# Feed-forward layers rebuilt: up projection by seven block products, hidden values through DRAM, down projection as a stage summed in PSUM

## The chip, the cores and the metric

The kernel runs on one core of a Trainium2 chip. The metric is device time in microseconds, the median of the runs; lower is better. Inputs and outputs are float32 in DRAM.

## What is computed

A two-layer model over 1024 tokens and 256 context tokens, width 1024. Each layer is a mixer (layer 0: gated recurrence and attention; layer 1: differential attention over both sets of tokens), an output projection with a gated residual, and a convolutional feed-forward network with a gated residual. The context tokens leave the model after the mixer of layer 1. The feed-forward network (hidden width 2816, that is 22 tiles of 128) is what is changed:

```python
def conv_ffn(u, w_up, conv_w, conv_b, w_down):
    a, g = jnp.split(u @ w_up, 2, axis=-1)
    g = dwconv(g, conv_w, conv_b, FFN_PAD)
    return (jax.nn.gelu(g) * a) @ w_down
```

The convolution has three taps along the tokens. `u` is the normalized, modulated residual stream; the modulation of layer 1 is itself a product of a condition vector with a 1024 x 6144 matrix, worked out in twelve chunks of 512 columns.

## The kernel before

All products of float32 values are made of float32r parts: a value is split into a high part (a cast) and a low part (the difference), and `mm3` (L113) issues three matmuls, high x high, low x high, high x low, each with a stationary operand of 128 x 128 and up to 512 moving columns. A weight unit is 128 x 1024: `unit` (L100) loads it on the SP queue into one of three `wr` buffers, casts it on POOL (`wh`) and takes the difference on DVE (`wl`).

`ffn` (L846) runs once for each layer and works on chunks of tokens whose normalized columns lie in SBUF: in layer 0 tokens 0 to 639 and then the other 640 (384 tokens and the context), in layer 1 two chunks of 512. The gate has one or two columns more in a first chunk, for the convolution. In each chunk a loop goes over eleven groups of two hidden tiles. `up(f)` loads and splits the unit of the gate and that of the value, and makes `pg` and `pa` in PSUM, each by 8 x 3 matmuls for each piece of columns; a piece has at most 512 columns, so 640 columns are two pieces of 320, 514 are 258 and 256, and 512 are one. The gate is copied by ACT, convolved in three DVE steps, passed through gelu on ACT and multiplied by `pa`; the hidden value is split into `hh` and `hl` in SBUF. `down(gi)` then multiplies the two hidden tiles with their two units of the down weights for each token tile, into `dps`; DVE multiplies that by the gate row (`dtmp`, L952), and POOL adds it to the residual tile `ht` (L953). So each token tile is evicted eleven times in a chunk. Between groups stand chunks of layer 1's modulation (`mod_chunk_dve`, L168) and the norms of the tiles of the next chunk.

`out_proj` (L767) goes before each: for each token tile 48 matmuls into `ops`, the DVE product `tmp` (L802), the POOL addition, and, three or four tiles behind in the text, the norm: `scaled` (L233: a square on ACT, a few small steps on DVE and POOL, a POOL product `xn`) and `turned` (L242: eight transposes on PE, five evictions on DVE and three on ACT). It norms only the tokens of the first chunk; the others are normed inside `ffn`. `layer1_front` (L977) follows the first `ffn`; in it the first five token tiles have their columns already.

A planner orders the instructions of these parts by their due times. Only the attention loops (L750, L1258) stand under `manual_schedule()`: there each engine and the SP queue run in the order of the text. SP issues all DMAs named here, one after another: an issue that waits holds up those behind it.

## Time and profile before

| what | us |
|---|---|
| median of three runs | 3431.25 |
| the runs | 3423.64, 3431.25, 3432.63 |
| span of the profiled execution | 3428.6 |
| busy: TensorE matmul, VectorE, GpSimd, ScalarE | 3283.1, 2523.3, 1741.2, 1097.8 |
| mean granted TensorE clock, share of full speed | 0.989 |

For the profiled execution the page gives the span alone, from its first instruction to its last; it has no time of its own beside the three runs. The span is 2.65 us under their median. The span is read in stages: about 440 us of layer 0's projections, attention to 738, output projection to 864, feed-forward to 1810, layer 1's projections to 2154, attention to 2574, output projection to 2684, feed-forward to the end. TensorE's busy time counts matmuls that overlap; what a stage costs TensorE is read from the distance between the starts of successive matmuls.

### The profile page before, as it was taken

How to read it: one execution, taken by the hardware profiler on the slowest of the kernel's cores; microseconds unless marked ns; L12 is line 12 of the kernel's file. 1: busy time of each engine (PE TensorE's matmuls, PEld its weight loads, DVE VectorE, ACT ScalarE, POOL GpSimd, SP SyncE). 2: the span in 40 equal slices, each digit the busy share in tenths (PEclk: the TensorE clock that was granted, in tenths of full speed). 3: DMA queues.
4: the chain of work that ended last, by engine and by line, in shares of the span. 5: the costliest groups of instructions: out<-in, count | busy, mean ns of one | idle time of the engine just before them, and what ended most of it. 6: DMA issues, size and time to landing. Idle time of an engine off the chain costs nothing.

```text
span 3428.6 us, 48308 instructions
## 1 busy us (share of the span) xinstructions
PE 3283.1 (96%) x18390; PEld 2840.4 (83%) x18390; DVE 2523.3 (74%) x3518; ACT 1097.8 (32%) x2126; POOL 1741.2 (51%) x1104
## 2 busy tenths in 40 slices
PE   8998989989999999999999999888889999999999
PEld 4877778877999999999997877677778888888887
DVE  6468978876777877666676784899987567677665
ACT  3355766732111111111122221677663111111010
POOL 2223578864445555445543332477773456554545
PEclk9999999999999999999999999999999999999999
DMA  7224953354523334333335445543404433333231
GB/s 260 71 75 126 290 141 94 89 149 153 178 93 111 111 99 166 107 104 108 110 110 182 121 123 142 140 128 97 135 29 169 148 101 103 102 126 105 93 98 68
DMA packets 218494, 424.41 MB, mean 124 GB/s; under 512 B 19948, under 2 KB 137708, under 8 KB 216472
## 3 DMA queue, kind: packets, MB, share of 16 engines
q1 hardware_dynamic: 216104, 413.47, 39.3%
q10 hardware_dynamic: 2160, 7.87, 0.7%
q8 instruction: 145, 2.38, 0.3%
q14 instruction: 85, 0.70, 0.1%
HBM read 335.88 MB, written 85.39 MB: 123 GB/s over the span
## 4 chain that ended last, share of the span: by engine, by line
PE 74%; DVE 15%; issue 4%; POOL 3%; DMA 2%; ACT 1%; SPq 0%; DVEq 0%; POOLq 0%; ACTq 0%
PE pg L118 5%; PE pg L117 5%; PE pg L116 5%; PE pa L117 5%; PE pa L118 5%; PE pa L116 5%; PE dps L118 5%; PE dps L117 5%; PE dps L116 5%; DVE m L1189 3%; DVE p L1205 3%; PE pj L116 3%; PE pj L118 3%; PE pj L117 3%; DVE tt L1203 2%
## 5 line engine op out<-in xcount | busy, mean ns | idle before, releaser
L90 POOL TENSOR_SCALAR wh<-wr 128x1024 fp32r<-128x1024 f32 (+3 forms) x328 | 398.7, 1222 | 763.1 <-issue 182.9
L953 POOL TENSOR_TENSOR ht<-ht,dtmp 128x1024 f32<-128x1024 f32 x197 | 506.8, 2581 | 205.9 <-DVE dtmp L952 203.7
L98 DVE TENSOR_TENSOR wl<-wr,wh 128x1024 fp32r<-128x1024 f32 (+2 forms) x328 | 505.9, 1554 | 101.1 <-POOL wh L90 101.0
L116 PE MATMUL pg<-u,wh 128*128 128x320 f32 (+4 forms) x1232 | 387.6, 315 | 0.0
L118 PE MATMUL pg<-u,wh 128*128 128x320 f32 (+4 forms) x1232 | 386.7, 314 | 0.0
L117 PE MATMUL pg<-u,wl 128*128 128x320 f32 (+4 forms) x1232 | 386.5, 314 | 0.0
L952 DVE TENSOR_TENSOR dtmp<-dps,ga 128x1024 f32<-128x1024 f32 x199 | 241.0, 1215 | 164.7 <-PE dps L118 137.0
L117 PE MATMUL pa<-u,wl 128*128 128x320 f32 (+1 forms) x1056 | 356.8, 338 | 0.0
L118 PE MATMUL pa<-u,wh 128*128 128x320 f32 (+1 forms) x1056 | 356.4, 337 | 0.0
L116 PE MATMUL pa<-u,wh 128*128 128x320 f32 (+1 forms) x1056 | 355.9, 337 | 0.0
L118 PE MATMUL dps<-wl,hh 128*128 128x512 f32 x792 | 309.4, 391 | 0.0
L117 PE MATMUL dps<-wh,hl 128*128 128x512 f32 x792 | 309.2, 390 | 0.0
L116 PE MATMUL dps<-wh,hh 128*128 128x512 f32 x792 | 308.7, 390 | 0.0
L98 POOL TENSOR_TENSOR wl<-wf,wh 128x1280 fp32r<-128x1280 f32 x64 | 221.7, 3465 | 105.8 <-ACT wh L1224 94.4
L1184 PE MATMUL S<-k,q 128*128 128x512 f32 (+1 forms) x768 | 196.4, 380 | 57.5 <-ACT p L1195 56.1
L911 ACT COPY g<-pg 128x64 f32<-128x64 f32 (+5 forms) x176 | 61.8, 406 | 576.8 <-PE pg L118 576.8
L116 PEld LDWEIGHTS pg<-u,wh 128*128 128x128 f32 x1232 | 231.8, 188 | 10.6 <-issue 1.7
L117 PEld LDWEIGHTS pg<-u,wl 128*128 128x128 f32 x1232 | 232.2, 189 | 9.0
L118 PEld LDWEIGHTS pg<-u,wh 128*128 128x128 f32 x1232 | 231.9, 188 | 7.8
L118 PEld LDWEIGHTS pa<-u,wh 128*128 128x128 f32 x1056 | 198.6, 188 | 15.7
L117 PEld LDWEIGHTS pa<-u,wl 128*128 128x128 f32 x1056 | 199.0, 188 | 15.0
L116 PEld LDWEIGHTS pa<-u,wh 128*128 128x128 f32 x1056 | 198.3, 188 | 14.5
(344 smaller groups left out, 8067.2 us busy)
## 6 DMA issues: line engine op xcount, KB each, us to landing
wr<-ffn_up SPq DMA_DIRECT2D x176, 512.0 KB
wr<-ffn_down SPq DMA_DIRECT2D x88, 512.0 KB
wr<-w_mod SPq DMA_DIRECT2D x76, 512.0 KB
k<-dk SPq DMA_DIRECT2D x14, 1280.0 KB
wr<-w_in_c SPq DMA_DIRECT2D x24, 512.0 KB
mr<-w_mod SPq DMA_DIRECT2D x20, 512.0 KB
dv<-vst SPq DMA_DIRECT2D x20, 512.0 KB
dk<-qT SPq DMA_DIRECT2D x80, 128.0 KB
```

The lines of the kernel that those rows point to most:

```text
L90: nc.gpsimd.tensor_scalar(out, x, 1.0, 1.0, op0=MUL, op1=MUL)
L98: e.tensor_tensor(out, x, hi.bitcast(F32), op=SUB)
L116: mm(out, a[0], b[0], start=start, stop=False)
L117: mm(out, a[1], b[0], start=False, stop=False)
L118: mm(out, a[0], b[1], start=False, stop=stop)
L911: nc.scalar.copy(g[:, o + lo - src:o + hi - src], pg[:, b, lo - c0:hi - c0])
L952: nc.vector.tensor_mul(tmp[:, c], ps.rearrange("p a b -> p (a b)")[:, c], gas[t0 >= SEQ][:, c])
L953: (nc.vector if last else nc.gpsimd).tensor_tensor(hts[i][:, c], hts[i][:, c], tmp[:, c], op=ADD)
L1184: nc.tensor.matmul(Y["S", m][:, c0:c0 + n], heads[h]["q"][m][:, t * P:(t + 1) * P], heads[h]["k"][x, m, j], start=(x == 0), stop=(x == 1))
L1189: nc.vector.tensor_reduce(Y["m", m], Y["S", m][:, :TOK], axis=AX.X, op=ALU.max, negate=True)
L1203: nc.vector.scalar_tensor_tensor(Y["tt"], s0[:, h, t:t + 1], self.nlam, Y["r"], op0=MUL, op1=MUL)
L1205: nc.vector.scalar_tensor_tensor(Y["p", 0], Y["p", 1], Y["tt"], Y["p", 0], op0=MUL, op1=ADD)
```

## The change

The feed-forward network becomes two stages in each layer, both wholly under `manual_schedule()`, with the hidden values of all tokens in DRAM (`hid_d`) between them.

- `out_proj` now norms every token tile. The 1024 tokens' columns are kept in float32 as four quarters `V` (half of the model's rows by half of the tokens); the context's columns are split at once (`uc`), and in layer 0 the context's tiles come first.
- `up_context` (layer 0 only) makes the hidden tiles of the 256 context tokens in the plain way, 48 matmuls of 256 columns for each. It reads all 44 units of the up weights.
- `operands` makes seven right-hand operands from the quarters, four of them by subtraction, and splits them. In layer 0 this work is handed out in pieces of 512 columns, three after each of the context's hidden tiles from the fifth on; in layer 1 in pieces of 2048 columns, in `up_begin`.
- `up_sequence` makes each hidden tile of the 1024 tokens by seven products of 12 matmuls of 512 columns (before: eight times that many columns' worth). The left-hand operands are sums of halves of the two weight units (`up_sums`, DVE). The products add up in three pairs of PSUM banks, between them ACT copies a partial sum out of the bank. The hidden tile goes to `hid_d`. In layer 0 seven chunks of layer 1's modulation stand in it.
- `ffn_down` goes over rounds of token tiles (layer 0: four, three, three; layer 1: four, four) whose sums stay in PSUM over all 22 hidden tiles. For each hidden tile it loads the unit of the down weights and the tile's tokens from `hid_d`, and splits both; three loads are ahead. A token tile is evicted once, at the end of its round. In layer 0's second and third round stand the other five chunks of modulation and the norms of the first seven tiles for layer 1.
- Both stages split weights on ACT (cast) and DVE, not POOL. `wr` has four buffers, not three; the other users of `wr` follow. `mod_chunk_dve` asks for its next load before it uses the last one. `mrow` has one buffer, not two. `layer1_front` finds seven tiles' columns made, not five.

The core of the diff (the old `ffn` is removed whole; `convolved` is its convolution, over up to 1024 columns, and `mod_steps` its modulation in six steps a chunk):

```diff
-AHEAD = 1
+NWR = 4
...
+    def place_columns(self, context):
...
+        self.V = {(i, j): pool.tile([P, 4, 512], F32, tag=f"v{i}{j}", name="v") for i in range(2) for j in range(2)}
...
+    def operands(self, U, T, n):
...
+        for k in range(0, 4, n):
+            ks = slice(k, k + n)
+            raw = {x: self.V[i][:, ks] for x, i in (("11", (0, 0)), ("12", (0, 1)), ("21", (1, 0)), ("22", (1, 1)))}
...
+            def sub(out, a, b, raw=raw):
...
+                    nc.vector.tensor_sub(raw[out], raw[a], raw[b])
...
+            def split(x, raw=raw, ks=ks):
+                return lambda: self.split(raw[x], *(y[:, ks] for y in hl[x]))
+            work += [sub("t1", "12", "11"), split("11"), sub("t2", "22", "t1"), split("t2"), split("t1"), sub("t3", "22", "12"),
+                     split("t3"), split("21"), sub("t4", "21", "t2"), split("t4"), split("22")]
...
+    def fetch_up(self, l, f):
...
+        for i in (f, NF + f):
+            raw = self.W.tile([P, 1024], F32, tag="wr", bufs=NWR, name="wr")
+            self.nc.sync.dma_start(raw, self.io["ffn_up"][l, i])
...
+    def split_new(self, x, pool=None, tag="w", bufs=4):
...
+        hi, lo = ((pool or self.W).tile([P, n], F32R, tag=tag + y, bufs=bufs, name="w" + y) for y in "hl")
+        self.split(x, hi, lo)
...
+    def ffn_up(self, l, chunks):
...
+            with self.tc.manual_schedule():
...
+                work = self.operands(U, self.sb(s2, f"sums{l}", side="right"), 4 if l else 1)
+                if l == 0:
...
+                        self.up_context(l, PS, self.sb(s3, f"upc{l}"), work)
+                    s2.close()
...
+                begun = self.up_begin(l, B, work)
...
+                    s2.close()
...
+                mods = [step for ch in chunks for step in self.mod_steps(F, 1, ch, 2 if ch < 4 else 1)]
+                self.up_sequence(l, PS, B, F, begun, mods)
+    def up_context(self, l, PS, F, work):
...
+        raws = {f: self.fetch_up(l, f) for f in range(2)}
+        w = {0: [self.split_new(x) for x in raws.pop(0)]}
...
+        def product(name, x):
...
+            for k in range(KT):
+                self.mm3(ps, [y[:, k * P:(k + 1) * P] for y in x], [y[:, k, :] for y in self.uc], k == 0, k == KT - 1)
...
+        def last(f):
+            gc, pa = part.pop(f)
+            nc.vector.tensor_mul(gc, gc, pa)
+            nc.sync.dma_start(self.hid_d[f, :, SEQ:], gc)
+        for f in range(NF):
+            a, g = w.pop(f)
+            pg = product("B", g)
+            nc.scalar.copy(gp[:, 1:1 + n], pg)
+            pa = product("E", a)
+            if f + 1 < NF:
+                w[f + 1] = [self.split_new(x) for x in raws.pop(f + 1)]
...
+            self.convolved(l, f, gp, gc, n)
+            part[f] = gc, pa
+            if f:
+                last(f - 1)
+            if f + 2 < NF:
+                raws[f + 2] = self.fetch_up(l, f + 2)
+            for _ in range(3 if f >= 4 else 0):
...
+        last(NF - 1)
...
+    def up_sums(self, B, raws):
...
+        nc.vector.tensor_add(s[:, 0], b[:, h], b[:, h2])
+        nc.vector.tensor_sub(s[:, 1], a[:, h], b[:, h])
+        nc.vector.tensor_sub(b[:, h], s[:, 0], a[:, h])
+        nc.vector.tensor_sub(s[:, 2], a[:, h2], b[:, h])
...
+    def up_begin(self, l, B, work):
...
+        raws = [self.fetch_up(l, f) for f in range(2)]
+        L = {"a": self.split_new(raws[0][0])}
+        some(2)
+        L["raw"] = self.up_sums(B, raws[0])
+        some(1)
+        L["g"] = self.split_new(raws[0][1])
+        some(1)
+        L["s"] = self.split_13(L["raw"])
+        some(7)
+        return L, raws[1]
+    def up_sequence(self, l, PS, B, F, begun, mods):
+        nc, right = self.nc, self.right
...
+        def product(out, x, c, n, first):
+            for k in range(4):
+                self.mm3(out, [y[:, c + k * P:c + (k + 1) * P] for y in x], right[n][k], first and k == 0, k == 3, not first)
...
+        for f in range(NF + 1):
+            Y, L = step.pop(f - 1, None), left.get(f)
+            if L:
+                X = step[f] = {x: bank(x) for x in "BEA"}
+                product(X["B"], L["a"], 0, "11", True)
+            if Y:
+                nc.scalar.copy(g[:, 1:513], Y["B"])
...
+            if L:
+                if f:
+                    L["s"] = self.split_13(L["raw"])
+                X["p"] = part(B, "p", X["B"])
+            if Y:
+                self.convolved(l, f - 1, g, gc, SEQ)
+                product(Y["E"], left.pop(f - 1)["s4"], 0, "22", False)
+                nc.vector.tensor_add(Y["a"][:, h2], Y["x"], Y["E"])
+                nc.vector.tensor_mul(gc, gc, Y["a"])
+                nc.sync.dma_start(self.hid_d[f - 1, :, :SEQ], gc)
...
+            L["s4"] = self.split_new(L["raw"][:, 2], F, "s4", 1)
+            product(X["B"], L["g"], 0, "t2", False)
+            X["x"] = part(F, "x", X["B"])
+            product(X["E"], L["s"], 0, "t1", True)
+            some_mods()
+            if f + 1 < NF:
+                left[f + 1] = {"a": self.split_new(raws[f + 1][0]), "raw": self.up_sums(B, raws[f + 1])}
+            product(X["B"], L["s"], 512, "t3", False)
+            y = part(F, "y", X["B"])
+            nc.vector.tensor_add(g[:, 513:1025], y, X["E"])
+            some_mods()
+            product(X["A"], L["a"], 512, "21", True)
...
+            nc.vector.tensor_add(X["a"][:, h], X["p"], X["A"])
+            if f + 1 < NF:
+                left[f + 1]["g"] = self.split_new(raws.pop(f + 1)[1])
+            product(X["B"], L["g"], 512, "t4", False)
+            if f + 2 < NF:
+                raws[f + 2] = self.fetch_up(l, f + 2)
...
+            some_mods()
+    def mod_steps(self, pool, l, ch, nctx):
...
+        return [lambda: next(it, None)] * 6
+    def ffn_down(self, l, rounds, dst, chunks, after):
...
+            items = [(r, f) for r in range(len(rounds)) for f in range(NF)]
...
+            def fetch(i):
+                r, f = items[i]
+                w = self.W.tile([P, 1024], F32, tag="wr", bufs=NWR, name="wr")
+                nc.sync.dma_start(w, io["ffn_down"][l, f * P:(f + 1) * P, :])
...
+                x = F.tile([P, 512], F32, tag="hr", bufs=4, name="hr")[:, :n]
+                nc.sync.dma_start(x, self.hid_d[f, :, rounds[r][0] * P:rounds[r][0] * P + n])
...
+            def split(i):
...
+                self.split(x, *hs)
+                parts[i] = hs, self.split_new(w)
+            def columns(t, ht):
...
+                return [lambda: self.scaled(F, ht, xn, xn.rearrange("p (k c) -> p k c", c=P)),
+                        lambda: self.turned(xn, AB, v), lambda: self.split(v, *u)]
+            with self.tc.manual_schedule():
+                for i in range(3):
+                    fetch(i)
+                split(0)
+                for r, tiles in enumerate(rounds):
...
+                        if r == 1:
+                            extra = [step for ch in chunks for step in self.mod_steps(F, 1, ch, 1)] + extra
+                        for f in range(NF):
+                            i = r * NF + f
+                            if i + 3 < len(items):
+                                fetch(i + 3)
+                            if f == 8:
+                                for t in tiles:
+                                    hts[t] = F.tile([P, D], F32, tag="ht", bufs=8, name="ht")
+                                    nc.sync.dma_start(hts[t], self.hm_d[t])
+                            if i + 1 < len(items):
+                                split(i + 1)
+                            hs, w = parts.pop(i)
...
+                                for b in range(2):
+                                    self.mm3(acc[t][:, b, :], [x[:, j * P:(j + 1) * P] for x in hs],
+                                             [x[:, b * 512:(b + 1) * 512] for x in w], f == 0, f == NF - 1)
+                            if r:
+                                coming = sum(3 * len(x) for x in rounds[r:-1]) if after else 0
+                                for _ in range(-(-(len(extra) + coming) // (len(items) - i))):
...
+                                        extra.pop(0)()
+                        for t in tiles:
...
+                            for c in [slice(0, 512), slice(512, D)] if last else [slice(0, D)]:
+                                nc.vector.tensor_mul(tmp[:, c], acc[t].rearrange("p a b -> p (a b)")[:, c], gas[t >= NTX][:, c])
+                                (nc.vector if last else nc.gpsimd).tensor_tensor(hts[t][:, c], hts[t][:, c], tmp[:, c], op=ADD)
+                                nc.sync.dma_start(dst(t)[:, c], hts[t][:, c])
+                        if after and r + 1 < len(rounds):
+                            for t in tiles:
+                                extra += columns(t, hts[t])
...
+                    self.PS, self.fine = self.ps(s3, "psB"), False
+                    self.place_columns(True)
...
+                    self.out_proj(0, "w_out_ab", [*range(NTX, NT), *range(NTX)], self.yT0)
+                self.ffn_up(0, range(7))
...
+            self.ffn_down(0, [range(0, 4), range(4, 7), range(7, NT)], lambda t: self.h1_d[t], range(7, 12), columns)
...
+                    self.PS = self.ps(s3, "psC")
+                    self.place_columns(False)
...
+                    self.out_proj(1, "w_out_c", range(NTX), self.yT1, self.first["w"])
+                self.ffn_up(1, ())
+            self.ffn_down(1, [range(0, 4), range(4, NTX)], lambda t: out[0, t * P:(t + 1) * P, :], (), None)
```

## Rows read from the trace of the kernel before

**Rows 1.** The page: busy time of each engine over the span.

```profile
PE 3283.1 (96%) x18390; PEld 2840.4 (83%) x18390; DVE 2523.3 (74%) x3518; ACT 1097.8 (32%) x2126; POOL 1741.2 (51%) x1104
```

**Rows 2.** A window of feed-forward 1: us, sum, PE, PEld, DVE, ACT, POOL, PEclk, DMA share, GB/s.

```profile
3250.00:3300.00 50.00, 50.00 (x218) 40.65 (x217) 35.06 (x40) 6.72 (x11) 23.48 (x14) 1.00 0.34 110
```

**Rows 3.** Tiles pg and dps in either layer: counts, first and last start.

```profile
L116 PE MATMUL pg<-u,wh x704: 303/308/418, 864.5 to 1773.9; 128*128 128x320 f32 x132, 128*128 128x322 f32 x44
...
L118 PE MATMUL dps<-wl,hh x440: 388/389/400, 921.3 to 1810.0; 128*128 128x512 f32 x147
...
L116 PE MATMUL pg<-u,wh x528: 276/284/403, 2683.4 to 3394.2; 128*128 128x258 f32 x59, 128*128 128x256 f32 x59, 128*128 128x512 f32 x58
...
L118 PE MATMUL dps<-wl,hh x352: 389/389/400, 2729.2 to 3422.4; 128*128 128x512 f32 x176
```

**Rows 4.** Timeline of PE: start, length; first and last of four runs of equal matmuls.

```profile
1200.69 0.31 PE L116 MATMUL pg<-u,wh 128*128 128x320 f32 x1
...
1207.87 0.30 PE L117 MATMUL pa<-u,wl 128*128 128x320 f32 x1
...
2779.64 0.39 PE L116 MATMUL pa<-u,wh 128*128 128x512 f32 x1
...
2784.53 0.28 PE L116 MATMUL pg<-u,wh 128*128 128x258 f32 x1
...
2785.97 0.28 PE L116 MATMUL pg<-u,wh 128*128 128x258 f32 x1
...
3200.87 0.39 PE L116 MATMUL dps<-wh,hh 128*128 128x512 f32 x1
...
3205.88 0.39 PE L117 MATMUL dps<-wh,hl 128*128 128x512 f32 x1
```

**Rows 5.** A group of feed-forward 0: busy, mean ns, idle before it, releasers.

```profile
L953 POOL TENSOR_TENSOR ht<-ht,dtmp 128x1024 f32<-128x1024 f32 x104 | 263.9, 2548 | 119.7 <-DVE dtmp L952 119.3 <-POOL ht L953 0.3
```

**Rows 6.** Waits of the SP queue, 2250 to 2420 us: total, times, longest.

```profile
SPq L1172 <- ACT os L1170: 115.8, 14, 11.3
```

**Rows 7.** Timeline of SP and POOL: issues, and the two casts that wait for landings.

```profile
2344.13 0.80 SPq L1172 DMA_DIRECT2D do<-os  x2
...
1250.01 2.57 SPq L105 DMA_DIRECT2D wr<-ffn_up  x3
...
1253.66 1.05 POOL L90 TENSOR_SCALAR wh<-wr 128x1024 fp32r<-128x1024 f32 x1 [5.36 <-DMA wr<-ffn_up]
1255.04 1.85 POOL L90 TENSOR_SCALAR wh<-wr 128x1024 fp32r<-128x1024 f32 x1 [0.33 <-DMA wr<-ffn_up]
```

**Rows 8.** Groups by form: ACT casts, DVE differences, the convolution's shapes, a 256 product.

```profile
L261 ACT CAST u<-v 128x1024 fp32r<-128x1024 f32 x24 | 25.2, 1049 | 0.4
...
L98 DVE TENSOR_TENSOR xl<-xc,xh 128x1280 fp32r<-128x1280 f32 x4 | 6.0, 1492 | 5.8 <-POOL xh L90 5.8
...
L302 DVE SCALAR_TENSOR_TENSOR xc<-xr,cols,xc 128x255 f32<-128x255 f32 x8 | 3.8, 477 | 0.0
...
L933 DVE TENSOR_TENSOR hv<-gc,pa 128x256 f32<-128x256 f32 x22 | 9.1, 413 | 0.0
```

**Rows 9.** Timeline: a norm in the last projection, from its first DVE step.

```profile
2617.84 1.22 DVE L802 TENSOR_TENSOR tmp<-ops,ga 128x1024 f32<-128x1024 f32 x1 [1.70 <-PE ops L118]
2618.99 1.68 DVE L251 TENSOR_SCALAR v<-ntp,A,B 128x128 f32<-128x128 f32 x5
...
2626.74 1.12 POOL L240 TENSOR_SCALAR xn<-tmp,rs_y 128x1024 f32<-128x1024 f32 x1 [2.97 <-DVE yms L1291]
```

**Rows 10.** Timeline of PE and one window behind its longest wait.

```profile
2488.03 1.22 PE L1184 MATMUL S<-k,q 128*128 128x512 f32 x2 [7.54 <-ACT p L1195]
...
2492.25 0.41 PE L1165 MATMUL po<-wl,v 128*128 128x256 f32 x1
...
2493.53 0.41 PE L1165 MATMUL po<-wl,v 128*128 128x256 f32 x1
...
2489.00:2494.00 5.00, 5.00 (x23) 4.65 (x22) 3.44 (x4) 3.52 (x6) 3.33 (x2) 0.50 0.00 0
```

335 lines of the change are left out of this document (157 added, 178 removed).

## The prediction

> **What bounds the kernel now.** I read the busy times first: TensorE 96% of the span, VectorE far behind [rows 1]. Then a window inside a feed-forward stage: TensorE busy 50.00 of 50 us at clock 1.00, VectorE 35 [rows 2]. So there, TensorE alone sets the time. The tiles' first and last starts give the stages: layer 0 from 864.5 to 1810, some 946 us; layer 1 from 2683.4 to 3422.4, 739 us [rows 3]. Last the distance from start to start of equal matmuls [rows 4]: 320 columns (1207.87 − 1200.69)/49 = 0.1465 us; 512 columns of the up product (2784.53 − 2779.64)/21 = 0.233; 256 or 258 columns (2785.97 − 2784.53)/12 = 0.12; 512 columns of the down product (3205.88 − 3200.87)/22 = 0.2277. The POOL additions, 104 of 2548 ns in layer 0 [rows 5], delayed no matmul, so taking them away gives nothing by itself.
>
> **1. TensorE's own work.** Before, layer 0: 22 hidden tiles × 2 chunks × 2 units × 24 matmuls × 2 pieces = 4224 × 0.1465 = 618.8 us up; down 22 × 10 tiles × 2 × 3 = 1320 × 0.2277 = 300.6. Layer 1: 1584 of 512 columns × 0.2329 = 368.9, 1056 of 257 × 0.12 = 126.7, down 1056 × 0.2277 = 240.5. After: the sequence is 22 × 84 = 1848 matmuls × 0.2277 = 420.8 in each layer, the context 1056 × 0.12 = 126.7 in layer 0; down as before. Layer 0 gains 618.8 − 547.5 = 71.3, layer 1 495.6 − 420.8 = 74.8: **−146.1 us**, if the new stages run as densely. I take 0.2277 since each operand is again 128 x 128 against 512 columns; at 0.2329 the 3696 matmuls cost 19 us more (rival D).
>
> **2. The context stage.** TensorE needs 48 × 0.12 = 5.76 us a hidden tile. But the text forms a loop. SP takes its instructions in order and, in such a block, holds at one that waits: in an attention loop it stood 115.8 us, in 14 waits of up to 11.3, at the write L1172 [rows 6]. In the new loop the write of f−1 waits for VectorE's product, VectorE has first to do the splits of f+1 and the convolution of f, and the pair of loads for f+2 stands behind the write. These splits wait for the loads that were asked for one turn before. So only one pair is under way, and a turn is load, split, convolution, product, load. Its lengths: the casts of a pair issued from 1250.01 on began at 1253.66 and 1255.04 [rows 7], so the second unit has landed 5.0 us after the first issue; the write ahead of them takes the queue about 0.4 (two issues in 0.80, [rows 7]) and a hop 0.1, an estimate. The last unit's cast takes 1.05, its difference 1.2 [rows 8, 9], the convolution three steps of at most 0.48, about 1.35, the product 0.41 [rows 8], hops between engines some 0.4. Together 5.5 + 1.05 + 1.2 + 1.35 + 0.41 + 0.4 = 9.9 us. The stage: 13.7 for the first tiles, 19 × 9.9, 5.8 for the last = 207.6 against 126.7: **+81 us**. Bounds: with loads that don't wait, a turn is VectorE's own work: two differences 2.44, convolution 1.35, product 0.41, three operand pieces of 512 columns at about 0.68 (from 1280 at 1.49), 0.6 for hops, 6.85 us (+23 for the stage); with landings 1.5 us slower, 11.4 (+110). I take 9.9, the row of the same size of load. The operands' pieces come after the loads in the text and lie in this idle time.
>
> By the Trainium skill, page "DMA: Bandwidth & Descriptors", section "Anatomy of one DMA — SWDGE (gpsimd) path", a transfer takes about 2.0 us and its bytes at 436 GB/s: 4.4 us for the pair, an estimate from that page's fit for another issuing path. By it a turn would be 9.3 us and the stage 12 us shorter; the row measures this kernel's queue, so the sum keeps 5.0.
>
> TensorE waits some 4 us of each turn there, and that may lower its clock: behind a wait of 7.54 us the granted clock was 0.50, the 1.2 GHz level, and a 256-column matmul took (2493.53 − 2492.25)/6 = 0.213 us [rows 10]. At this clock a turn is 48 × 0.213 = 10.25 us of TensorE, hardly over 9.9: +7 us at most, kept for the range.
>
> The Trainium skill says, in "TensorE: Matmul & The Clock Gate", section "Why this matters for your kernels", that matmuls between long DMA waits run cold. The row above agrees for a wait on ACT; no row of before shows a feed-forward block that waits on loads. By the rule these 7 us are due, and the sum would end at 3457.
>
> **3. From the context to the sequence, layer 0.** Before the first product stand a fetch, the casts and differences of the first pair, the sums; then the partial sum `p` is copied by ACT behind the casts of the gate and the sums: **+10 us**, between 4 (load already landed) and 16.
>
> **4. Start of the sequence in layer 1.** Nothing of the context hides the operands here. The last projected tile must be normed and turned: from its VectorE product at 2617.84 to the end of POOL's `xn` 10.0 us in before [rows 9]; without the work of other tiles beside it I count 7.7, then transposes and evictions, 10.5 after the last product in all. Then VectorE does four subtractions and seven differences of 2048 columns. By 1.22 us for 1024 [rows 9] and 1.49 for 1280 [rows 8] that is 2.3 each, 25.3; the sums and splits of the first pair add 6.4: 31.7 us. ACT's seven casts of about 1.9 (from 1.05 for 1024, [rows 8]) go beside them, but the copy of `p` stands behind the last, and the second product into that bank waits for it. Five products of 12 × 0.2277 = 2.73 and their copies follow, so the first tile's six products end 46.5 us after the operands can start. Of that 6 × 2.73 = 16.4 are TensorE's own, counted in 1. So 10.5 + 46.5 − 16.4 and 3 us at half clock = **+43.5 us**, between 14 (if the norms of the first half let the operands start early, and products run behind each split) and 55.
>
> **5. Seams and extra steps.** In the steady sequence a turn is 19.15 us of TensorE; VectorE has 13.6 us in it, up to 19.6 with two modulation steps, ACT 7: no term. Down: each item's loads are three items ahead, 12 matmuls more a tile than VectorE needs: no term in the steady part. Left are the projection's end in layer 0 (+2), from up to down twice with the first load of hidden values behind the last write (+8 in all), three round ends at which PSUM must be evicted before its reuse (3 × 3), modulation and norm steps of PE, DVE and ACT in the down rounds that no longer have a slack of a whole group (+9), modulation in up (+2), a tail that evicts four tiles rather than one (+2.5): 32.5, less 2 in `layer1_front`, which finds seven tiles made: **+30.5 us**, between 5 and 60. No row of before shows these steps; the values are single evictions, casts and landings at 1 to 5 us each. The fourth `wr` buffer, the casts on ACT and the single `mrow` lie beside TensorE: nothing, as long as ACT has its 7 of 19 us.
>
> **Sum.** −146.1 + 81 + 10 + 43.5 + 30.5 = +18.9 us. On the span of 3428.6 that is 3447.5; the median of the runs lies 2.65 above this span, so **3450 us**.
>
> **Rivals.** A, faster: the loads of the context stage aren't held by the write (SP's order is not binding across them, or the pair lands in the time of one). Then a turn is 6.85 us, 58 us fall away: about 3392. For it speaks that several loads were under way at once on this queue in before; against it the 115.8 us at L1172. B, faster: layer 1's start overlaps the projection, since the operands from the first half's tokens are ready tiles earlier. 30 us less: 3420. Against it: the first subtraction needs the second half's quarter, and VectorE's order is that of the text. C, slower: the seams don't overlap. Down's first read of `hid_d` waits until the last hidden tile has been evicted, multiplied, written and landed, and no TensorE work stands between: about 11 us at each of two seams, with some 3 of half clock: +28, 3478. It decides if the first down matmul comes more than 8 us after the last up matmul. D, slower: the matmuls of the sequence, whose operands change every time as before, keep the up product's 0.2329: +19, 3469. That the change doesn't do what it says I exclude by its text: the count of matmuls is fixed.
>
> **How the numbers follow.** The forecast 0.42, with its own range of 3422 to 3480 (the context's bounds of some −12 and +7, the starts' and seams' −15 to +20); A 0.22, B 0.14, C 0.13, D 0.09. The range from 3380 to 3485 takes in A, whose lower part and the slowest of C stay out. About 0.3% (10 us, 3421 to 3441.5) is what a measurement can tell from no change. Faster: A, 0.09 of B and 0.03 of the forecast: 0.34. Within: 0.05 of B and 0.11 of the forecast: 0.16. Slower: 0.28 of the forecast, C and D: 0.50.
>
> **What would show it.** Right: starts of 512-column matmuls in the sequence 0.228 apart; a context turn of 9 to 11 us with VectorE and ACT waiting for `wr` and SP for the product; a gap of TensorE of 30 us or more at layer 1's up start; both down stages dense. Wrong: context turns under 8 us (A), the first product of layer 1's sequence early with no long gap behind it (B), a gap of 10 us at up's end (C), distances of 0.233 (D). The whole would be wrong if VectorE set the pace of the sequence: turns above 19.5 us without modulation.

## The result and the profile after

The changed kernel took 3541.0 us (median of four runs, 3535.7 to 3547.9) against 3430.0 of the kernel before: a ratio of 1.0328, 95% interval 1.0311 to 1.0346. It is slower, as forecast, but by 111 us where the forecast said 19. The profiled execution has a span of 3533.9 us, 105.3 above the one before.

The page, busy time of each engine and the granted clock in 40 slices (PE is TensorE, PEld its weight loads, DVE VectorE, ACT ScalarE, POOL GpSimd; SP is the engine that issues the loads and writes):

```profile
PE 3210.9 (91%) x16262; PEld 2665.9 (75%) x16262; DVE 2398.2 (68%) x3393; ACT 1448.3 (41%) x2474; POOL 950.8 (27%) x658
...
PEclk9998989999888999999999999999999989999999
```

TensorE works 72 us less than in [rows 1] and the span is 105 longer: it now waits. Windows of 50 us (length, busy time of PE, PEld, DVE, ACT, POOL, then clock, DMA share, GB/s) show in which stages; [rows 2] answers to the second one:

```profile
1000.00:1050.00 50.00, 38.08 (x256) 36.04 (x254) 30.30 (x46) 20.68 (x31) 0.00 (x0) 0.86 0.38 122
...
1300.00:1350.00 50.00, 50.00 (x221) 41.21 (x221) 42.36 (x51) 17.58 (x24) 0.00 (x0) 1.00 0.32 106
...
1700.00:1750.00 50.00, 38.22 (x144) 30.25 (x143) 27.84 (x39) 10.96 (x16) 1.05 (x2) 0.84 0.72 231
...
2800.00:2850.00 50.00, 18.06 (x76) 13.76 (x74) 32.60 (x41) 18.83 (x24) 6.56 (x6) 0.68 0.13 42
```

In the context stage (first) TensorE is busy 38 of 50 us at clock 0.86; the sequence (second) is as dense as before; in the second round of layer 0's down stage (third) it is idle for 12 us of 50, around the start of layer 1's sequence (fourth) for 32. A sum by stages, from the first and last matmul of each tile, as in [rows 3]:

| stage | before | after | difference |
|---|---|---|---|
| start to layer 0's output projection | 738.4 | 763.0 | +24.6 |
| output projection 0 | 126.3 | 122.2 | −4.1 |
| feed-forward 0, to the first `pj` of layer 1 | 945.6 | 1042.2 | +96.6 |
| projections of layer 1 | 343.9 | 350.5 | +6.6 |
| attention and output projection of layer 1 | 529.4 | 531.3 | +1.9 |
| feed-forward 1 | 739.2 | 715.3 | −23.9 |
| tail | 5.8 | 9.4 | +3.6 |

Feed-forward 0 after is 15.9 us from the projection's last matmul to the context's first, 206.5 for the context, 6.1 to the sequence, 451.0 for it, 3.9 to down, 355.7 for down, 3.1 to `pj`.

### The profile page after: what moved, and what is told of

Same layout as the page of the kernel before. It is cut to its first block, busy times and chain, and to the rows that moved or that the text cites. A ratio compares the mean times of both kernels' runs of the same rounds, so it can differ in the third digit from the quotient of the medians.

```text
span 3533.9 us, 43650 instructions
## 1 busy us (share of the span) xinstructions
PE 3210.9 (91%) x16262; PEld 2665.9 (75%) x16262; DVE 2398.2 (68%) x3393; ACT 1448.3 (41%) x2474; POOL 950.8 (27%) x658
## 5 line engine op out<-in xcount | busy, mean ns | idle before, releaser
L117 PE MATMUL acc<-wh,hh 128*128 128x512 f32 x792 | 316.0, 399 | 14.4 <-ACT wh L273 10.6
L119 PE MATMUL acc<-wl,hh 128*128 128x512 f32 x792 | 315.1, 398 | 11.8 <-DVE wl L99 11.8
L118 PE MATMUL acc<-wh,hl 128*128 128x512 f32 x792 | 313.8, 396 | 2.8 <-DVE hl L99 2.8
L1168 POOL TENSOR_TENSOR ht<-ht,dtmp 128x1024 f32<-128x1024 f32 x17 | 42.0, 2508 | 928.0 <-DVE dtmp L1167 928.0
L273 ACT CAST wh<-wr 128x1024 fp32r<-128x1024 f32 x242 | 253.6, 1049 | 59.8 <-DMA wr<-ffn_up 37.4
L117 PE MATMUL pB<-ht,wh 128*128 128x512 f32 x528 | 207.2, 393 | 24.5 <-ACT p L1039 24.5
L119 PE MATMUL pB<-lt,wh 128*128 128x512 f32 x528 | 206.8, 392 | 0.0
L118 PE MATMUL pB<-ht,wl 128*128 128x512 f32 x528 | 206.7, 391 | 0.0
L117 PE MATMUL pj<-wh,u 128*128 128x512 f32 x448 | 179.2, 400 | 17.8 <-ACT u L273 8.6
L1388 DVE TENSOR_REDUCE m<-S 128x1 f32<-128x1280 f32 x128 | 187.0, 1479 | 6.6 <-PE S L1383 5.8
L118 PE MATMUL pj<-wh,u 128*128 128x512 f32 x448 | 179.0, 400 | 0.0
```

What stands on the lines that cost most here:

```text
L117: mm(out, a[0], b[0], start=start, stop=False, skip_group_check=onto)
L118: mm(out, a[1], b[0], start=False, stop=False, skip_group_check=onto)
L119: mm(out, a[0], b[1], start=False, stop=stop, skip_group_check=onto)
L273: self.nc.scalar.copy(hi, x)
L1168: (nc.vector if last else nc.gpsimd).tensor_tensor(hts[t][:, c], hts[t][:, c], tmp[:, c], op=ADD)
L1388: nc.vector.tensor_reduce(Y["m", m], Y["S", m][:, :TOK], axis=AX.X, op=ALU.max, negate=True)
```

## The experiments

They are read stage by stage, from the tiles' first and last starts, since the front of one and the same text moves by some 4 us between runs (attention in layer 0 starts at 454.7 to 458.9). The kernels e5_mrow1 and e12_all to e16_c4 were run two to ten times, the others once; a stage of these is read from one profile.

**The context stage, e1_ctx.** The loads stand ahead of the write:

```diff
-            if f:
-                last(f - 1)
             if f + 2 < NF:
                 raws[f + 2] = self.fetch_up(l, f + 2)
+            if f:
+                last(f - 1)
```

> Context stage: the pair of loads for f+2 is asked for ahead of the write of f-1, nothing else. Theory (the write holds the loads, so a turn is load + split + convolution + product): a turn falls from 9.8 us to about 6.9, the stage from 206.5 to about 149, the total by about 55 us. Rival (the landing of the loads, or VectorE's own work, is the length of a turn): a turn stays above 9 us and the total within 10 us.

In the changed kernel the mean turn, from a hidden tile's first `cB` matmul to the next tile's, is (1100.5 − 901.1)/21 = 9.5 us, 6.7 in the first two and 9.8 from the fourth on, and the waits of the SP queue and a timeline show the loop. The tile's row in the tile view (matmuls, ns least/median/most, first and last start):

```profile
L117 PE MATMUL cB<-uc,wh x176: 275/379/582, 901.1 to 1104.2; 128*128 128x256 f32 x176
```

The wait of the SP queue at the write, 920 to 1090 us (total, times, longest):

```profile
SPq L968 <- DVE gc L967: 141.9, 17, 8.9
```

One turn in the timeline (start, length, engine, line, what was waited for in brackets):

```profile
965.49 0.41 DVE L967 TENSOR_TENSOR gc<-gc,cE 128x256 f32<-128x256 f32 x1
...
965.93 0.33 SPq L968 DMA_DIRECT2D hid<-gc  x1
966.35 0.88 SPq L906 DMA_DIRECT2D wr<-ffn_up  x2
...
970.54 1.05 ACT L273 CAST wh<-wr 128x1024 fp32r<-128x1024 f32 x1 [1.30 <-DMA wr<-ffn_up]
971.77 1.04 ACT L273 CAST wh<-wr 128x1024 fp32r<-128x1024 f32 x1 [0.18 <-DMA wr<-ffn_up]
```

The product ends at 965.9, the write goes out at 965.93, the loads behind it at 966.35, and the casts of what they bring begin at 970.54 and 971.77. SP stood 141.9 us at the write. Two windows of the same turn show TensorE's granted clock (columns as above):

```profile
965.00:968.00 3.00, 3.00 (x16) 3.00 (x16) 2.27 (x6) 1.45 (x3) 0.00 (x0) 0.50 0.43 79
969.00:971.00 2.00, 2.00 (x20) 2.00 (x19) 0.00 (x0) 0.70 (x2) 0.00 (x0) 1.00 0.88 352
```

So the 0.86 of the long window is a mean of two levels. Behind the waits for casts and differences TensorE runs at 0.50, the 1.2 GHz level, for 3 to 6.5 us, in about half of the turns, and at 1.00 otherwise. With the loads first (e1_ctx), the same row of the tile view:

```profile
L117 PE MATMUL cB<-uc,wh x176: 276/279/562, 899.0 to 1052.1; 128*128 128x256 f32 x176
```

Most turns are 6.84 us (7.1 in the mean), the stage 156.4 (899.0 to 1055.4), 50 us less; the span fell to 3487.7. The loop was the price. But 6.84 us is not VectorE's work, as I had put it: VectorE is busy 109 of 145 us there (900 to 1045), and the first four turns, which hold no piece of the operands, take 6.7 to 6.9 as well. In the waits of e1_ctx, 920 to 1045 us, TensorE waits for the last split:

```profile
PE cB L118 <- DVE wl L99: 17.2, 18, 1.1
```

ACT's copy of the gate stands ahead of the casts of the next pair, so a turn is a gate product (2.9 us), copy, two casts, a difference. With the splits ahead of the copy too (in e12_all, e14_a3, e15_c3 and e16_c4) turns without operand pieces take 5.65 us, which is TensorE's own time.

**The modulation in the sequence, e3_copies.** In `mod_chunk_dve`, for two conditions:

```diff
+        if which not in (2, 5):
+            for c in range(nctx):
+                for j in range(4):
+                    nc.tensor.matmul(ps[c][:, j:j + 1], acc[c][:, j * P:(j + 1) * P], self.ones[:, 0:1],
+                                     start=True, stop=True)
+            for c in range(nctx):
+                nc.vector.tensor_copy(self.mcol[l][:, 4 * ch:4 * ch + 4, c], ps[c][:, 0:4])
+            return
         for c in range(nctx):
...
```

In the loop that follows, which the changed kernel uses for every chunk, the copy stands behind each condition's four matmuls.

> In a modulation chunk with two conditions the matmuls of both stand ahead of the two copies out of PSUM. Theory (TensorE waits 2.1 us for the copy between them, which stands behind other VectorE work, and the clock falls to 0.50 behind it): the four long turns of layer 0's sequence (26.2, 24.6, 23.0, 25.9 us) come to about 20.3, the total falls by about 18 us. Rival (the chunk's own VectorE work, four more steps of 0.68, makes these turns long): they stay above 22.5 us, the total within 6 us.

In the changed kernel, TensorE's timeline around such a chunk:

```profile
1166.49 0.95 PE L207 MATMUL modps<-ones,macc 128*128 128x1 f32 x8
1169.28 1.72 PE L207 MATMUL modps<-ones,macc 128*128 128x1 f32 x8 [1.84 <-DVE mcol L209]
...
1172.29 0.63 PE L117 MATMUL pA<-h,wh 128*128 128x512 f32 x1
1172.72 0.63 PE L118 MATMUL pA<-h,wl 128*128 128x512 f32 x1
```

The window behind it (columns as above):

```profile
1170.00:1175.00 5.00, 5.00 (x15) 4.13 (x16) 0.16 (x1) 0.00 (x0) 0.52 (x1) 0.50 0.00 0
```

The second condition's matmuls wait 1.84 us for the copy of the first, and behind this the granted clock is 0.50, the 1.2 GHz level: matmuls of 512 columns start 0.43 us apart. With the copies last (e3_copies), the same place in the timeline:

```profile
1163.71 1.84 PE L202 MATMUL modps<-ones,macc 128*128 128x1 f32 x16
```

The window behind it:

```profile
1165.00:1170.00 5.00, 5.00 (x25) 4.24 (x26) 3.04 (x7) 1.05 (x1) 0.78 (x2) 1.00 0.00 0
```

All sixteen matmuls run at once and the clock stays at 1.00. The four turns are 20.94 us each, from 26.16, 24.55, 22.97 and 25.93: 15.8 us less, of which the four waits themselves are 7.4. In other runs with this text unchanged the four turns add up to 99.6 to 102.8 us, so the gain is 16 to 19. The theory holds; the span is 3517.6.

**The modulation in the down rounds, e2_modsup, e6_mods11, e14_a3, e15_c3.** The first two move chunks, e6_mods11 with a third step a turn; the last gives the loads of the down rounds a ring of their own.

```diff
-                self.ffn_up(0, range(7))
+                self.ffn_up(0, range(12))
...
-            self.ffn_down(0, ..., range(7, 12), columns)
+            self.ffn_down(0, ..., (), columns)
```

In e6_mods11 these are `range(11)` and `range(11, 12)`, and one more `some_mods()` stands ahead of the last product.

> All twelve chunks of layer 1's modulation stand in layer 0's up sequence, none in the down rounds. Theory (in the down rounds the modulation's loads share the ring of four buffers with the down weights, and VectorE stands at them with the next splits behind it): the second round falls from 121 us to about 92, the sequence grows by 5 x 1.2 to 8 us, the total falls by 20 to 25 us. Rival (the rounds of three tiles are slow by their own loads and splits: 4.1 us of TensorE against 768 KB an item): the second round stays above 110 us and the total within 8 us.

The row of `acc` in layer 0, in the changed kernel and in e2_modsup:

```profile
L117 PE MATMUL acc<-wh,hh x440: 387/390/773, 1568.6 to 1923.4; 128*128 128x512 f32 x147
...
L117 PE MATMUL acc<-wh,hh x440: 387/389/792, 1630.2 to 1957.6; 128*128 128x512 f32 x147
```

To the end of its last matmul down took 328.3 us instead of 355.7, and its second round 104.4 instead of 121.6, between what theory and rival name. But the sequence has two steps a turn, 44 in all, and 28 of 72 ran alone behind it, in a gap of 67 us: 3569.6.

> The changed kernel with eleven chunks of modulation in layer 0's up sequence, three steps a turn, and one chunk in the down rounds. e2_modsup showed the down stage 27 us shorter, but a sequence with two steps a turn had no room for twelve chunks, and 28 steps ran alone behind it. Theory (the down stage pays for five chunks 27 us, the sequence hides their VectorE steps): down near 333 us, the sequence within 10 us of its 451, the total 15 to 22 us less. Rival (VectorE, with 13.6 us of its own in a turn of 19.1, becomes the bound when three steps stand in it): turns of 21 us and more over the whole stage, the total as before or longer.

Down took 329.8, but pairs of turns with two-condition chunks 48 us instead of 38, and the sequence 471.1 us instead of 448.2 (first to last `pB`): 3528.7. The loss had only moved: turns above 21 us, as the rival says, but in the first four chunks alone (20.5 us in the others). In the changed kernel, waits of VectorE and of SP in the second round:

```profile
DVE macc L193 <- DMA wr<-w_mod: 39.5, 14, 6.4
...
SPq L1110 <- DMA wr<-w_mod: 27.8, 10, 4.8
SPq L1110 <- DVE macc L193: 20.6, 14, 1.6
```

VectorE stands 39.5 us at the modulation's loads, with the splits of the next down unit behind it; SP stands 48 us ahead of the loads of down units, at loads of the modulation and at the VectorE steps that read them. e14_a3 has three buffers in this ring and no ring for the modulation:

> The changed kernel with three buffers in the ring, the loads and splits of the context stage asked for earlier, both conditions' modulation matmuls ahead of their copies, layer 1's first products behind their splits, and the projection's inputs on the other side as in e7_yleft; the modulation stays where the change put it, since e12_all gave back in the sequence (460 us, not 433) what it gained in down. Theory (the costs add up: 20, 60, 18, 12, 6): the span falls by some 115 us to 3410 to 3425, 0.2 to 0.6% faster than before. Rival (with three buffers the context's turn goes back to 8 us or more): 3430 or longer.

Waits of VectorE in the second round of e14_a3:

```profile
DVE macc L193 <- DMA wr<-w_mod: 51.5, 19, 6.0
```

Down took 370.0 us, its second round 137.6, VectorE's wait 51.5. Then, with a ring of its own for the down rounds (`own` is set there alone):

```diff
-            raw = self.W.tile([P, 1024], F32, tag="wr", bufs=NWR, name="wr")
+            raw = pool.tile([P, 1024], F32, tag="mr", bufs=3, name="mr") if own else self.W.tile([P, 1024], F32, tag="wr", bufs=NWR, name="wr")
...
+        ahead = [load(1)] if own else []
...
-            after = load(u + 1) if u < 3 else None
+            if own and u < 2:
+                ahead.append(load(u + 2))
+            after = (ahead.pop(0) if ahead else None) if own else load(u + 1) if u < 3 else None
```

> As e14_a3, and the modulation's loads in the down rounds have a ring of three buffers of their own and are asked for two ahead. Theory (what the five chunks cost in the second round is VectorE standing at their loads and the shared ring, not their work): the second round falls from 121 us to 95 to 105, the total by 15 to 25 us below e14_a3. Rival (the transfers themselves, 512 KB for each step beside 704 KB for each item of 4.1 us, are the limit): the second round stays above 115 us and the total within 6 us of e14_a3.

Waits of VectorE in the second round of e15_c3:

```profile
DVE macc L198 <- DMA mr<-w_mod: 16.1, 5, 6.1
```

The wait is 16.1 us, the second round 108.8, down 340.7, 29 less than in e14_a3, with the same transfers: the shared ring and the short distance of the loads were the cause of these 29, not the bytes. The two were changed together and aren't told apart. But 14 of the 29 only make up for what three buffers cost there (370.0 against 355.7). With four buffers and the modulation's own ring (e16_c4, below) the row reads

```profile
L117 PE MATMUL acc<-wh,hh x440: 387/389/796, 1473.9 to 1813.3; 128*128 128x512 f32 x147
```

that is 340.2 us for down, against 355.7 in the changed kernel and 328.3 without any chunk in it. So of the 27 us that the five chunks cost there, the ring and the distance explain 15, each within some 3 us: down stages without an edit took 352 to 358 us in the other runs. Of the 40 us left in e15_c3 over the matmuls' 300.6, some 18 lie in the third round, with the norms (turns of 4.08, 4.98 and 5.45 us instead of 4.10), 19 in the second, with the modulation and a round's end, and 3 in the first. In all 3393.5 us, a ratio to the kernel before of 0.9894 (0.9879 to 0.9908): 1.1% faster than it.

**The front, e5_mrow1, e9_ring, e10_ahead, e13_r3.** Attention in layer 0 began 22.8 us later than before, far ahead of the rebuilt stages. Three of these kernels edit the kernel before, e13_r3 the changed one.

```diff
e5_mrow1, e9_ring and e10_ahead
-        rows = self.S.tile([2, 512], F32, tag="mrow", bufs=2, name="mrow")
+        rows = self.S.tile([2, 512], F32, tag="mrow", bufs=1, name="mrow")
e9_ring also, here and at the other users of wr
-        raw = self.W.tile([P, 1024], F32, tag="wr", bufs=3, name="wr")
+        raw = self.W.tile([P, 1024], F32, tag="wr", bufs=4, name="wr")
...
e10_ahead also, in mod_chunk_dve
...
+            after = load(u + 1) if u < 3 else None
e13_r3
-NWR = 4
+NWR = 3
```

> The kernel before, with one buffer for the modulation's row instead of two. Theory (in the changed kernel the first projections of layer 0 end 23 us later because a chunk of modulation waits for the row of the chunk before it, and the order of the work shifts behind it): attention starts near 459 us, not 436, and the total grows by 20 to 25 us. Rival (the fourth buffer of the weight ring, or the loads of the modulation asked for one earlier, shift the order): attention starts within 5 us of 436, the total within 6 us.

> The kernel before, with four buffers in the ring of weight loads and one for the modulation's row (and one buffer less for an output tile of layer 1's attention, to make room). e5_mrow1 showed 5 of the 23 us by which layer 0's projections end later in the changed kernel. Theory (the fourth buffer lets more loads compete and the planner places the work otherwise): attention starts 12 to 23 us later than 436. Rival (the modulation's loads that are asked for one ahead do that): it starts within 6 us of 441.

> The kernel before, with one buffer for the modulation's row and with the modulation's loads each asked for one ahead, as in the changed kernel; three buffers in the ring. Theory (the fourth buffer is the cause of the late projections): attention starts within 6 us of the 441 of e5_mrow1. Rival (the loads asked for ahead are): it starts at 450 or later.

> The changed kernel with three buffers in the ring of weight loads instead of four, nothing else. e9_ring showed attention 20 us late in the kernel before with four. Theory (the fourth buffer is the cause of the late front, and the new stages don't need it): attention starts near 437 to 442, the total falls by 15 to 22 us. Rival (the new stages live on the fourth buffer): the front gains 20 us, but the context stage, the sequence or the down rounds lose as much, the total within 6 us of the changed kernel.

The tile view gives the first and last start of the score matmuls `S` of layer 0. In the kernel before:

```profile
L116 PE MATMUL S<-k,q x192: 281/398/763, 436.1 to 715.2; 96*128 96x512 f32 x128, 96*128 96x256 f32 x64
```

In the changed kernel:

```profile
L117 PE MATMUL S<-k,q x192: 278/397/767, 458.9 to 736.5; 96*128 96x512 f32 x128, 96*128 96x256 f32 x64
```

In e10_ahead:

```profile
L116 PE MATMUL S<-k,q x192: 361/398/796, 440.5 to 720.3; 96*128 96x512 f32 x128, 96*128 96x256 f32 x64
```

In e9_ring:

```profile
L116 PE MATMUL S<-k,q x192: 280/398/765, 456.8 to 735.9; 96*128 96x512 f32 x128, 96*128 96x256 f32 x64
```

In e13_r3:

```profile
L117 PE MATMUL S<-k,q x192: 278/398/766, 440.5 to 718.0; 96*128 96x512 f32 x128, 96*128 96x256 f32 x64
```

One row buffer: 441.4, and 3433.6 us against 3430.6 (ratio 1.0012, 1.0001 to 1.0023). With the loads ahead as well: 440.5. With the fourth ring buffer: 456.8, span 3456.3. The changed kernel with three: 440.5. So the fourth buffer delays the front, by 15 to 16 us in the kernel before, by 18 in the changed one and by 14 between e15_c3 and e16_c4 (below). The row buffer's 4 to 5 us are no more than the front moves by itself; the median grew by 3. In the changed kernel the fourth buffer also lengthens layer 1's projections (350.6 against 337.9 us). In e13_r3 the down stage gives 14 us back (369.4), which is most of why the span falls by 13.6 only and not by 31, to 3520.3 (median 3520.7, ratio 1.0264, 1.0244 to 1.0285). Both theory and rival hold, each for its stages. How more buffers make the planned front slower I did not find. Most of the delay arises at its end: from e10_ahead to e9_ring the last `pk` matmul moves from 418.0 to 429.8, the last `hT` from 432.2 to 451.7, while the last `latp` is 1.6 us later. TensorE's waits there spread over many tiles; among those that grew are POOL's `qs`, from 3.3 to 6.9 us, and VectorE's `vst`, new with 4.1.

**The gap ahead of the projection, e4_order, e7_yleft, e11_yo.** Between attention's last matmul (753.8) and the first of the projection (763.0) TensorE waits 9.2 us, which the kernel before does not. e11_yo has both edits.

```diff
e4_order
-                    self.out_proj(0, "w_out_ab", [*range(NTX, NT), *range(NTX)], self.yT0)
+                    self.out_proj(0, "w_out_ab", [*range(NT)], self.yT0)
e7_yleft
-            Y = self.sb(st, f"outy{l}", side="right")
+            Y = self.sb(st, f"outy{l}", side="right" if l else "left")
```

> Layer 0's output projection takes the tokens' tiles first and the context's last, as before the change. Theory (the first tile of the context is the one that attention writes last, so TensorE waits 9.5 us for its loads): the gap ahead of the projection goes, and the total falls by 8 to 10 us. Rival (the norms of the context's tiles, now last, delay the context stage by as much): the gap goes, but the context stage starts as late as before, the total within 3 us.

> The changed kernel with the buffers of layer 0's projection inputs (yr, yp, yh, yl) on the other side of SBUF, under those of the projection itself. e4_order left the 9.2 us ahead of the projection as they were, so the order of the tiles isn't their cause. Theory (the quarters, 48 KB with the context's columns, push these buffers onto memory that attention reads until its end, so their loads wait): the loads start 10 us and more ahead of attention's end, the gap falls under 2 us, the total by about 8. Rival (something else holds the loads, as the queue's order): the gap stays at 9 us.

> The changed kernel with the buffers of layer 0's projection inputs on the other side of SBUF and the tokens' tiles first, e4_order and e7_yleft together. Theory (each of the two was enough to hold the loads: the place of the buffers behind attention's last reads, and the context's tile behind attention's last writes): the gap ahead of the projection falls from 9.2 us to under 2, the total by 12 to 20 us. Rival (the order of the queue around the written-out block holds them): the gap stays above 8 us, and the total is that of e7_yleft.

The gap stayed in all three: 9.2, 9.4 and 9.1 us. All three theories fell. The tail of attention is 7.6 us shorter in the changed kernel (294.9 us from `S` to the last product, 302.5 before, where the queue issued the projection's loads within it), so the two nearly cancel and the gap costs some 2 us. Whether those loads are what lengthens the tail wasn't tried. Why the planner keeps these loads behind attention stays open. The span of e7_yleft is 11.5 us shorter (3522.4). Of this, 5.5 lie at the projection's other end: 10.4 us from the projection to the context, not 15.9. Another 3.8 lie in the front, which moves by as much in any run.

**The start of layer 1, e8_early.** The first tile's products are issued in `up_begin` right behind their splits; `x` and `y` lie in a buffer of the ring.

```diff
         some(2)
+        product(X["B"], L["a"], 0, "11", True)
         L["raw"] = self.up_sums(B, raws[0])
...
+        self.nc.scalar.copy(X["p"], X["B"])
         some(1)
+        product(X["B"], L["g"], 0, "t2", False)
...
```

> The changed kernel with the first hidden tile's products each right behind the split of its operand, and the copies out of PSUM between the casts rather than behind the last one. Theory (in layer 1 the copy of p behind the last cast holds five products of 2.73 us): the first tile's six products end about 13 us earlier, the gap of 24.2 us breaks into shorter ones, the total falls by 11 to 14 us. Rival (the row of VectorE's differences alone sets the first turn, and the second hidden tile waits for the last of them anyway): the first turn shrinks by less than 5 us.

In the changed kernel, TensorE's wait, 2809 to 3280 us:

```profile
PE pB L117 <- ACT p L1039: 23.8, 1, 23.8
```

ACT's timeline at it:

```profile
2848.92 1.90 ACT L273 CAST ht<-v 128x2048 fp32r<-128x2048 f32 x1 [5.14 <-DVE v L893]
2850.72 1.89 ACT L273 CAST h<-v 128x2048 fp32r<-128x2048 f32 x1
2852.52 0.58 ACT L1039 COPY p<-pB 128x512 f32<-128x512 f32 x1
```

The copy of `p` comes at 2852.52, behind the cast of the last operand, though its product ended near 2829. In e8_early the first turn is 33.3 us instead of 47.3, the second 21.5; layer 1's sequence is 11.7 us shorter, and the theory holds. In layer 0, where the context hides the operands, the sequence came out longer with the same edit (455.6 us against 448.2, first to last `pB`; unedited ones of other runs reach 451), so later kernels keep it to layer 1.

**Whether the costs add up, e12_all, e14_a3, e16_c4.** e12_all holds the edits of e1, e3, e6, e8 (layer 1 alone), e4 and e7, and in the context stage also:

```diff
             a, g = w.pop(f)
+            if f + 1 < NF:
+                w[f + 1] = [self.split_new(x) for x in raws.pop(f + 1)]
             pg = product("B", g)
```

> The changed kernel with: the loads of the context stage ahead of the write and the splits of f+1 ahead of the copy of f; both conditions' modulation matmuls ahead of their copies; eleven chunks of modulation in the up sequence; layer 1's first products behind their splits; the projection's inputs as in e11_yo. Theory (the costs found are separate and add up: 52 and 20 in the context stage, 18, 20, 12, 12): the span falls by 125 to 150 us, to some 3385 to 3410, that is 0.6 to 1.3% faster than the kernel before. Rival (VectorE, in a turn of the sequence with three steps of modulation, and the late front take it back): no faster than before, 3430 or more.

Span 3435.0 in the fastest of four runs, median 3451.3, ratio 1.0066 (1.0049 to 1.0083): the context took 141 us, but eleven chunks made the sequence 460.5, where e3_copies has 432.5, and gave back what down gained, and the late front stayed. The rival holds. e14_a3 leaves out e4 and e6 and takes three buffers: 3423.4 us, ratio 0.9980 (0.9970 to 0.9989). Its span is 113.3 below the changed kernel's: front 19.6, context 66.1, sequences 15.1 and 8.1, the norms ahead of the context and of layer 1's sequence 8.8, layer 1's projections 10.9, less 14.4 in down, 114 in all. So these parts add up to the difference between the two kernels, and the theory of e14_a3 holds.

> As e15_c3, but with four buffers in the ring of the weights. Theory (the fourth buffer costs 20 us in layer 0's front and brings nothing in the new stages once the modulation has its own ring): 17 to 23 us longer than e15_c3. Rival (the down rounds or the context stage need it): within 8 us of e15_c3.

e16_c4 differs from e15_c3 in the fourth buffer alone: span 3413.1 against 3392.8 (medians 3422.6 and 3393.5), with 14.2 more at attention's start and 11.7 more in layer 1's projections; feed-forward 0 is 3.5 shorter, down in it the same (340.2, 340.7). With a ring of its own for the modulation the new stages gain no more than that from the fourth buffer.

## Why the prediction was too small

**Right: the matmuls.** Turns of the sequence are 19.13 us, 84 × 0.2277, in both layers (rival D falls); down items of four tiles 5.44, as 24 × 0.2277 (5.46). The −146.1 is there.

**Right: the context's loop.** Forecast +81, measured 206.5 − 126.7 = +79.8. The casts began 4.2 and 5.4 us behind the first issue, where the forecast put the second landing at 5.0. The bound of 6.85 was right in size only: the loop through ACT sets it, not VectorE. Rival A falls for the changed kernel, and e1_ctx is what it described. An estimate from the fit in the Trainium skill, "DMA: Bandwidth & Descriptors", section "Anatomy of one DMA — SWDGE (gpsimd) path", for another issuing path, was 4.4 us for the pair and 9.3 for the turn. The trace has 5.4 and, from the fourth turn on, 9.8, so the row was the better price.

**Right: the starts.** From context to sequence 6.1 us and 3.6 in the first turn, +9.7 for +10. Layer 1: 13.1 from the projection to the first product and 30.9 in the first turn (47.3 less the six products' 16.4), +44.0 for +43.5, with ACT's copy where the prediction put it; rival B falls. The seams from up to down are 3.9 us each, and rival C falls.

**Wrong: "nothing" for the fourth buffer and the row buffer.** They were costed within the rebuilt stages, as lying beside TensorE, and the reason named there, ACT's 7 of 19 us, concerns the casts alone. But the ring serves every stage: attention began 22.8 us later, some 14 to 18 of them by the fourth buffer, and layer 1's projections, with seven tiles' columns made, took +6.6 instead of −2 (a fourth buffer's 12.7 in it). By which waits the buffer does this stays open.

**Wrong: the down rounds.** 355.7 us less 1320 × 0.2277 = 300.6 leaves 55, where the prediction had 9 for steps and about 6 for round ends. The step said that no term lies in the steady part since loads are three items ahead. Two things were left out. The modulation costs 27 of the 55 (e2_modsup): its loads share the ring, are asked for only one ahead, and VectorE, in text order, stands at them with the splits behind; a ring of its own, with loads two ahead, gives back 15. The walk along a queue that the prediction made for the write of the context stage was not made for these loads. The other 28 stay when no chunk is in the rounds: norms and round ends. No run takes the norms out, so their share is read from the turns alone.

**Wrong: modulation in up.** +2 forecast, 26.4 measured (the excess of seven chunks' turns over 19.13), of which 15.8 come from the copy between the two conditions and the clock behind it, by e3_copies. The row for this was [rows 10]: a wait that drops the clock costs more than its length. Here four waits of 1.8 us cost 2.0 to 5.2 each. In the context stage the clock fell as well, to 0.50 for 3 to 6.5 us behind the waits, but TensorE was idle for 12 of 50 us beside it and the loop of loads set the turn, so the 7 us kept for the range were not due. The Trainium skill says in "TensorE: Matmul & The Clock Gate", section "Why this matters for your kernels", that matmuls between long DMA waits run cold. The context stage agrees, with its 0.50 behind the waits for loads; the 0.50 in the sequence came behind a shorter wait that is no DMA's.

**Wrong: layer 0's projection end.** +2 forecast, 15.9 measured. The norm of the last tile, 10.0 us in [rows 9], was charged in layer 1 alone. The transposes of that tile stand ahead of the context's first product on TensorE, although the context doesn't need them; TensorE waits 10.5 us for `xn`. No run moves them, so this is read from the trace alone.

Against these, the stages of before held 26.2 and 3.1 us beyond their matmuls (945.6 − 919.4, 739.2 − 736.1), among them the same modulation and norms; the sum left that out, which hid some of the rest.

The sum forecast 18.9 us on the span and 105.3 came: 86 short. That is 20.5 up to the end of layer 0's output projection, 13.9 at that projection's end, 24.4 for modulation in up, 40 in layer 0's down rounds, 8.6 in layer 1's projections, and 5 in small differences, less the 26.2 of before. The paths that were walked through step by step (the context's loop, the two starts, the seams) came out within 3 us; what failed was entered as a round number for "seams and steps", or as nothing. The direction says little for the prediction: it gave "slower" a chance of 0.50.

## What to carry to other kernels

Cost a change of a shared resource (a ring of buffers, a staging row) in every stage that uses it, not only in the stage that it was made for. Where the order of each engine is the text's, each load must be asked for ahead of every instruction that waits, and side work (here modulation) does better with a ring and a distance of its own, or its landing holds the main work behind it; here that gave back 15 of the 27 us that the side work cost. Walk through the steps that look small as carefully as the big one: four waits of 1.8 us between two groups of small matmuls cost 15.8 us, with what the clock lost behind them. And read the clock in short windows: 0.86 over 50 us was 0.50 and 1.00 in turns.

## What the runs showed of the hardware

A wait of 1.84 us on TensorE, between two groups of eight one-column matmuls in otherwise dense work, was followed by at least 5 us at a granted clock of 0.50; with the copies last, the sixteen matmuls without the wait were followed by 1.00. In the context stage, which waits in every turn, the granted clock changed between 0.50, for 3 to 6.5 us behind about half of the waits, and 1.00; over 50 us this reads as 0.83 to 0.86. Pairs of 512 KB loads issued 0.44 us apart reached their casts after 4.2 and 5.4 us.
